# A scheduler's duration table, two groups of side work placed later, and the value products of stick-breaking attention issued for two query blocks at a time

## The chip, the cores and the metric

The kernel runs on one core of a Trainium2 chip. The metric is the device time of one execution in microseconds (us), given as the median of the runs shown. Five instruction streams matter: TensorE (PE in the profile, with its weight loads as PEld), VectorE (DVE), ScalarE (ACT), GpSimd (POOL) and SyncE (SP), whose queue carries most of the loads.

## What is computed

A sequence of 1024 tokens of width 1024, in float32, goes through three layers. Layer one is a short convolution with gates. Layer two is stick-breaking attention with 16 heads of 64, in query blocks of 128:

```
z = einsum(q, k) * inv_sqrt_d ;  mask = kpos < qpos          # strictly below
log_beta = log_sigmoid(z) ;  log_1m_beta = where(mask, log_beta - z, 0)
suffix = cumsum(log_1m_beta, reverse) - log_1m_beta
a = where(mask, exp(log_beta + suffix), 0) ;  out = a @ v
```

Layer three is a block with two attentions side by side, a sliding window (8 heads) and a differential attention (4 heads, two softmaxes each, a norm behind), merged by gates, and a feed-forward part with a convolution and a Gelu. Each layer has shifts, scales and gates that come from a vector-matrix product with a conditioning vector (`c @ w`); layer three has six of them in `w_ada` (1024 x 6144): `shift1, scale1, gate1, shift2, scale2, gate2`. The first three are used around the attentions, the last three around the feed-forward part.

## The kernel before, in words

Activations are kept transposed (channels on the partitions) in two halves of 512 tokens. Each large product is made of three TensorE passes over a high and a low part of both operands. A weight piece (128 x 512) is loaded by SP (`wr`), its high part is cast on ACT (`wh`), its low part is a subtraction on DVE (`wl`); an activation tile gets its high part on ACT and its low part on DVE (`split_to`). The products write PSUM tiles `pj` (`pv` where the tokens stand on the partitions).

The order on every engine is fixed when the program is built, by a planner (`Sched`). The main line calls one projection after another (`run_q0`, `run_bo0`, ...) and these are TensorE's filler. Everything else is a side task, a Python generator, that yields what it waits for; `turn` lets the side tasks whose time has come put their instructions in between. Time is the planner's own: `note` (line 153) adds to a clock for each engine a duration worked out from the operation and its width. So a duration in `note` changes no instruction but moves many. `until(cond)` runs side tasks alone, without filler, until a condition holds. Flags such as `"attn2"` live in the planner only; on the chip there are the semaphores that follow from the data.

Side tasks that matter here:

- `stick` (line 1068): a unit is one head of a head pair p and one query block i; with n = i+1 key blocks. It multiplies scores (`z`), takes two sigmoids on ACT (`om`, `be`, or `ob` for both where n is at most 4), a scan on DVE over `om` (a running product), a product of `be` and `om` on DVE, n transposes on TensorE (`tr`), copies on ACT (`aT`), and then, when both heads of the pair are there, the products with the values into `o`: 64 columns of the array for each head, key blocks 0 to i, the last one (the diagonal) with 127 rows instead of 128. The units of half 0 (i = 0 to 3) run beside `run_q0` to `run_z1a`, those of half 1 (i = 4 to 7) beside `run_bo0`, `run_z1`, `run_c0`, `run_g0`. `until(("stick", 0))` stands ahead of `run_bo0`.
- `swa` and `diff`: the two attentions of layer three. A unit of `diff` makes two softmaxes (a custom DVE instruction that adds the distance and reduces, shown as CUSTOM_DVE_ANT_0 in the trace and ISA in the order; an exponential on ACT), combines them on DVE (`p`), transposes, multiplies. After the fourth block of a head comes a norm (`sub_norm`: `sq`, `sm`, a square root on ACT, `rb`) and the split of `od`. `until(("attn2", 1))` stands ahead of `run_br1`, the first projection that reads `od` of half 1; `run_g1` and `run_up0` are the filler before it.
- `gemv_side`: the products with the conditioning vector, a load `mw` on SP and an accumulation `acc` on DVE for each 128 x 512 piece. For `w_ada` that is 96 pieces, one per 1.8 us of planned time (`EVERY`), in one go.
- `combine`: sums and differences of the tiles of two halves (`T`, `xn`) ahead of `run_up1`.
- `act_side`: loads (`al`) and splits of the down projection's inputs, from the start of `run_up1` on.
- `weight_sums`: adds blocks of weights by DMAs on the POOL queue.

Of the kernel before, what the change touches and what calls it, by code (L numbers as in the profile page):

```python
# [16 lines left out]
D = 1024  # L17
S = 1024
HT = 512
# [24 lines left out]
N_SP = 8  # L44
T_XT = 55.0
EVERY = 1.8
N_Z = 2
N_G = 7
M_BR = 5
# [8 lines left out]
class Sched:  # L58
# [91 lines left out]

        self.in_bank[ap.tensor.name][0] = None

    def note(self, eng, op, out, args, extra=0.0):
        ready = self.ready
        names = [a.tensor.name for a in args]
        self.seq += 1
        start = max([self.clk[eng]] + [ready.get(n, 0.0) for n in names])
        o = out.tensor.name
        n = out.free_size()
        lat = 0.1  # L160
        if eng == "pe":
            start = max(start, self.fresh.pop(o, 0.0))
            if op == "transpose":
                d = 0.113 if self.t > 30.0 else 0.213
            elif args[0].dtype == F32R:
                d = n / 2400 if n >= 256 else n / 600
            elif args[0].dtype == BF16:
                d = n / 2400
            elif n == 1:
                d = 0.2 if self.t > 30.0 else 0.37  # L170
            else:
                d = n / 600 if args[0].free_size() == 128 else n / 1070
            d += 0.0026
        elif eng == "act":
            d = n / 1400 + 0.155 + extra
        elif eng == "dve":
            fast = op in ("tensor_scalar", "tensor_copy") and all(a.space == out.space != bass.MemoryType.PSUM
                                                                  for a in args)
            d = n / (1920 if fast else 960) + 0.06
            if op == "reciprocal":  # L180
                d += n / 192
        else:
            d = 1.05 if eng == "pool" else 0.55
            nbytes = n * out.shape[0] * 4
            t = max(self.clk["dma"], start + d) + nbytes / 360e3
            self.clk["dma"] = t
            lat = t + 1.8 - start - d
        self.clk[eng] = start + d
        for nme in names + [o]:
            self.last[nme] = self.seq, max(start + d + lat, self.last.get(nme, (0, 0.0))[1])  # L190
        ready[o] = max(ready.get(o, 0.0), start + d + lat) if eng != "pe" else start + d + lat
        if eng != "pe":
            for nme in names:
                b = self.in_bank.get(nme)
                if b is not None:
                    b[0] = max(b[0] or 0.0, start + d)
# [29 lines left out]
class Engine:  # L226
# [5 lines left out]
    def __getattr__(self, op):  # L232
        f = getattr(self.eng, op)

        def call(out, *value, **kw):
            if op == "activation":
                s = Sched.SETS.get(kw["func"])
                if s and s != self.sch.set:
                    self.sch.set = s
                    self.sch.clk["act"] += 1.28  # L240
            args = [a for k, a in kw.items() if isinstance(a, bass.AP) and k not in ("accum_out", "identity")]
            extra = 0.19 * any(isinstance(kw.get(k), bass.AP) for k in ("scale", "bias")) + 0.095 * ("accum_out" in kw)
            self.sch.note(self.name, op, out, args, extra)
            if "accum_out" in kw:
                self.sch.ready[kw["accum_out"].tensor.name] = self.sch.ready[out.tensor.name]
            if self.dry:
                return None
            if op in ("matmul", "memset"):
                return f(out, *value, **kw)  # L249
            return f(out=out, **kw)  # L250
        return call
# [13 lines left out]
def tile_body(  # L265
# [802 lines left out]
    def stick(live, half, width, rho):  # L1068
        nk = (half + 1) * HT
        kv, qs = stick_in[half]  # L1070
        st = {}

        def work(p, i, h):
            yield from arrived(kv, p)
            yield from arrived(qs, p)
            n = i + 1
            w = n * 128
            kk, vt, q = kv[p][0][h], kv[p][1], qs[p][h]
            yield kk, q
            qb = q[:, :, (i % 4) * 128:(i % 4 + 1) * 128]  # L1080
            yield from room(1 if w <= HT else 3, int(w > HT))
            if w <= HT:
                both = big([2, HT], name="ob")
                om, be = both[:, 0, :], both[:, 1, :]
            else:
                om, be = big([D], name="om"), big([D], name="be")
            for c0, c1 in CUTS[n]:
                yield from sch.a_bank()
                ps = bank("z")
                o = ps[:, 0:c1 - c0]  # L1090
                mm(o, lhsT=qb[:, 0, :], rhs=kk[:, c0:c1], start=True, stop=False)
                mm(o, lhsT=qb[:, 1, :], rhs=kk[:, c0:c1], start=False, stop=True)
                e = min(c1, w)
                act(out=om[:, c0:e], in_=ps[:, 0:e - c0], func=ACTF.Sigmoid, scale=-1.0)
                act(out=be[:, c0:e], in_=ps[:, 0:e - c0], func=ACTF.Sigmoid)
            yield om


            rev = om[:, 0:w][:, ::-1]
            vec.tensor_tensor_scan(out=rev, data0=rev, data1=cst1["begin"][:, D - w:D][:, ::-1], initial=0.0, op0=ALU.mult,  # L1100
                                   op1=ALU.add)
            vec.tensor_tensor(out=be[:, 0:w - 1], in0=be[:, 0:w - 1], in1=om[:, 1:w], op=ALU.mult)
            free(w > HT)
            yield be
            aT = yield from turn(be, n)
            free()
            got = st.setdefault((p, i), {})
            got[h] = aT
            if len(got) < 2:
                return  # L1110
            if p not in st:
                yield from sch.a_bank()
            if p not in st:
                st[p] = [bank("o"), 0]
            po = st[p][0]
            yield vt
            for kb in range(n):
                r = slice(0, 127 if kb == n - 1 else 128)
                for hh in range(2):
                    mm(po[64 * hh:64 * hh + 64, (i % 4) * 128:(i % 4 + 1) * 128],  # L1120
                       lhsT=vt[r, kb * 128 + 64 * hh:kb * 128 + 64 * hh + 64],
                       rhs=got[hh][r, kb * 128:(kb + 1) * 128], start=kb == 0, stop=kb == n - 1)
            free(2 * (w > HT))
            del st[p, i]
            st[p][1] += 1
            if st[p][1] == 3 and ("z", p, half) in flags:
                zs[p, half] = sml(name="zl")
                syn.dma_start(out=zs[p, half], in_=z_d[p, :, hs(half)])
            if st[p][1] == 4:
                o = sml(name="o")  # L1130
                z = zs.get((p, half))
                if z is None:
                    vec.tensor_copy(out=o, in_=po)
                else:
                    vec.tensor_tensor(out=o, in0=po, in1=z, op=ALU.mult)
                if z is not None and in_use[0] + R_OB <= N4:
                    flags.add(("oB", p, half))
                    sch.spawn(split_to(("oB", p, half), o))
                else:
                    store(o_d[p, :, hs(half)], o)  # L1140
                del kv[p], qs[p], st[p]
                free(3 + 2 * half)
                kv["done"].add(p)
                qs["done"].add(p)

        yield from crew(live, [(p, i, h) for p in range(8) for i in range(4 * half, 4 * half + 4) for h in range(2)],
                        work, width, lambda p, i, h: rho * 0.32 * (i + 1), lambda: flags.add(("stick", half)))
# [295 lines left out]
            combine("h2", "T", rb, xs, GS["2"], V["sh2"], 6.0)  # L1443

    def h2_side():
        while "f" not in RB:
            yield 1.0
        for j in range(NJ):
            sch.spawn(from_dram(x4_d, 0, j, RB["f"], GS["2"][:, j:j + 1], V["sh2"][:, j:j + 1], ("h2", j, 0)))
# [590 lines left out]
    with tc.manual_schedule():  # L2040
# [135 lines left out]
        def mods_2():  # L2176
# [6 lines left out]
                yield 1.0  # L2183
            V["f_conv_n"] = const.tile([128, 3 * NF], F32, name="f_conv_n")
            vec.tensor_scalar(out=V["f_conv_n"], in0=V["f_conv"], scalar1=-1.0, scalar2=None, op0=ALU.mult)
            yield from gemv_side(w_ada_2[0], 0, 6 * D, sc2, mod_2, V["b_ada"], EVERY)
            make_gs("1", "sc1", "n1_g")
            make_gs("2", "sc2", "n2_g")
            vec.tensor_scalar(out=V["gt1"], in0=V["gt1"], scalar1=0.5, scalar2=None, op0=ALU.mult)
            flags.add("mods_2")  # L2190

        def consts_2():

# [88 lines left out]
        sch.spawn(ob_load(1))  # L2282
        run_bo1()
        run_g0b()
        run_c1()
        sch.until(lambda: ("attn2", 0) in flags)
        run_br0()
# [6 lines left out]
        run_up0b()  # L2294
        run_wo1()
        run_up0c()
        sch.spawn(act_side())
        run_up1()
        ahead.update(load=AHEAD_LOAD + E_L, h=AHEAD_H + E_H, l=AHEAD_L + E_H)
        run_last()  # L2300
# [33 lines left out]
```

## Time and profile before

| what | value |
|---|---|
| median of 3 runs | 2584.52 us (2581.15 to 2585.07) |
| the profiled execution's own time | 2582.41 us |
| its span, first to last instruction | 2580.6 us |
| PE busy | 2505.5 us (97%) |
| DVE, ACT, POOL busy | 1792.8, 1255.7, 490.0 us |
| mean granted TensorE clock | 0.991 |

PE is busy nearly all the time, so the places where it is not are few and can be listed one by one. [...] In a row of the waits the engine on the left sat idle until the one behind the arrow was done. [...]

### The profile page before, as it was taken

To read this page: it belongs to the slowest core of one execution; us is meant where nothing else is said; L and a number is where in the kernel's file an instruction comes from. 1 tells how busy PE (TensorE), PEld (TensorE's weight loads), DVE (VectorE), ACT (ScalarE), POOL (GpSimd) and SP (SyncE) were. 2 spreads that over 40 slices of the span, in tenths; PEclk is the share of its full clock that TensorE was granted. 3 is DMA by queue.
4 is the path that set the end of the run, shared out by engine and by line. 5 is a ranking of instruction groups with operands and counts; after the bars stand their busy time and mean duration, and the time that the engine had idled before them with its cause. 6 is when DMAs were issued, how large, how long until landed. Compare 5 with 4: busy or idle time off the path is not lost.

```text
span 2580.6 us, 38805 instructions
## 1 busy us (share of the span) xinstructions
PE 2505.5 (97%) x13215; PEld 2057.5 (80%) x13215; DVE 1792.8 (69%) x3245; ACT 1255.7 (49%) x2529; POOL 490.0 (19%) x894
## 2 busy tenths in 40 slices
PE   7999999989999899998999999999999899999998
PEld 6888888879877677787888887888888678788887
DVE  7866666777697788986765556774666876677555
ACT  5311112555455677677664353564634634345442
POOL 0012112312101002331211321222222222221000
PEclk9999999999999999999999999999999999999999
DMA  9867869857897665775876978977886987978764
GB/s 283 264 190 201 203 214 280 235 185 249 279 274 222 204 163 157 221 192 140 250 217 160 262 209 261 260 226 220 200 237 217 237 225 235 238 225 252 226 201 130
DMA packets 541726, 570.43 MB, mean 221 GB/s; under 512 B 32910, under 2 KB 410008, under 8 KB 541528
## 3 DMA queue, kind: packets, MB, share of 16 engines
q1 hardware_dynamic: 482644, 381.99, 50.3%
q0 software_dynamic: 56528, 181.75, 25.3%
q10 hardware_dynamic: 2356, 4.21, 0.4%
q8 instruction: 104, 1.70, 0.3%
q14 instruction: 94, 0.77, 0.1%
HBM read 466.90 MB, written 186.91 MB: 253 GB/s over the span
## 4 chain that ended last, share of the span: by engine, by line
PE 65%; DVE 5%; DMA 3%; ACT 2%; issue 2%; SPq 0%; POOL 0%; DVEq 0%; ACTq 0%; POOLq 0%
PE pj L249 53%; PE o L249 4%; PE z L249 4%; PE tr L250 3%; DVE om L250 2%; PE pv L249 1%; DMA wr<-sg_d2g 1%; DVE be L250 1%; DVE wl L250 1%; DMA wr<-in_b_w_out_dram 1%; DVE ob L250 1%; DVE act L250 0%; DVE fa L250 0%; ACT om L250 0%; ACT be L250 0%
## 5 line engine op out<-in xcount | busy, mean ns | idle before, releaser
L249 PE MATMUL pj<-act,wh 128*128 128x512 f32 (+1 forms) x5680 | 1783.0, 395 | 26.2 <-DVE act L250 16.8
L249 PEld LDWEIGHTS pj<-act,wh 128*128 128x128 f32 x5680 | 1046.2, 189 | 256.8 <-DVE act L250 22.9
L249 PE MATMUL pj<-act,wl 128*128 128x512 f32 (+1 forms) x2840 | 1113.7, 392 | 0.0
L249 PEld LDWEIGHTS pj<-act,wl 128*128 128x128 f32 x2840 | 536.2, 189 | 123.1 <-DVE wl L250 1.3
L250 DVE TENSOR_TENSOR wl<-wr,wh 128x512 fp32r<-128x512 f32 x714 | 476.4, 679 | 169.7 <-ACT wh L250 156.2
L250 ACT CAST wh<-wr 128x512 fp32r<-128x512 f32 x714 | 425.8, 617 | 177.6 <-PE pj L249 41.8
L250 POOL COPY paced<-wl 128x1 f32<-128x1 f32 x256 | 114.7, 448 | 881.6 <-DVE wl L250 840.9
L250 ACT COPY aT<-tr 128x512 f32<-128x512 f32 (+3 forms) x272 | 128.7, 501 | 162.0 <-PE tr L250 159.6
L249 PE MATMUL z<-kd,qs 128*128 128x512 f32 (+2 forms) x704 | 166.4, 350 | 1.7 <-DVE o L250 0.7
L250 DVE SCALAR_TENSOR_TENSOR acc<-mw,silu_c,acc 128x512 f32<-128x512 f32 x196 | 146.5, 748 | 2.7 <-DMA mw<-in_a_mod_w_dram 0.3
L249 PEld LDWEIGHTS z<-kd,qs 128*128 128x128 f32 x704 | 113.7, 190 | 19.4 <-issue 7.2
L250 DVE TENSOR_TENSOR_SCAN om<-om,begin 128x640 f32<-128x640 f32 (+3 forms) x64 | 120.6, 1885 | 10.2 <-ACT om L250 10.2
L249 PEld LDWEIGHTS o<-aT,vp 128*64 128x64 f32 (+2 forms) x1440 | 99.9, 149 | 22.8 <-issue 14.5
L249 PE MATMUL o<-aT,vp 128*64 128x128 f32 (+2 forms) x1440 | 116.3, 280 | 0.4 <-ACT aT L250 0.4
L250 ACT COPY u<-pj 128x512 f32<-128x512 f32 x46 | 27.0, 588 | 157.8 <-PE pj L249 80.1
L250 ACT ACTIVATE p<-p,t 128x256 f32<-128x256 f32 (+7 forms) x128 | 81.3, 636 | 20.7 <-DVE t L250 20.5
L250 ACT ACTIVATE sq<-xn 128x512 f32<-128x512 f32 x48 | 30.6, 637 | 110.6 <-DVE xn L250 110.5
L250 ACT ACTIVATE om<-z 128x384 f32<-128x384 f32 (+2 forms) x128 | 69.3, 542 | 22.6 <-PE z L249 19.0
L249 PE MATMUL pj<-wh,act 128*128 128x256 f32 x448 | 79.9, 281 | 0.0
L250 PE MATMUL tr<-ident,be 128*128 128x128 f32 x416 | 61.1, 283 | 18.1 <-DVE be L250 17.7
L250 PEld LDWEIGHTS tr<-ident,be 128*128 128x128 f32 x416 | 47.3, 143 | 32.4 <-DVE be L250 20.7
L250 DVE TENSOR_TENSOR be<-be,om 128x639 f32<-128x639 f32 (+3 forms) x64 | 66.2, 1034 | 6.7 <-ACT sq L250 0.5
(252 smaller groups left out, 2757.5 us busy)
## 6 DMA issues: line engine op xcount, KB each, us to landing
wr<-in_w_in_dram SPq DMA_DIRECT2D x136, 256.0 KB
mw<-in_w_ada_dram SPq DMA_DIRECT2D x96, 256.0 KB
wr<-in_a_w_in_dram SPq DMA_DIRECT2D x80, 256.0 KB
al<-dn_d SPq DMA_DIRECT2D x77, 256.0 KB
wr<-in_w_up_dram SPq DMA_DIRECT2D x66, 256.0 KB
sw_d<-in_w_down_dram POOLq DMA_DIRECT2D x48, 352.0 KB, 5.0
wr<-in_b_w_qz_dram SPq DMA_DIRECT2D x64, 256.0 KB
qs<-q_d SPq DMA_DIRECT2D x64, 256.0 KB
```

Source lines behind the costliest of these rows:

```text
L249: return f(out, *value, **kw)
L250: return f(out=out, **kw)
```

## The change

Four edits. (1) In `note` the scan costs n/470 + 0.04 us instead of n/960 + 0.06, a `scalar_tensor_tensor` with a scalar from memory 0.068 us more, a `tensor_tensor_reduce` (the custom instruction) 0.03 us more. (2) `w_ada` is taken in two goes: the first three vectors as before, the last three after the flag `attn1` (set behind `run_g0b`), one piece per 3.0 us. (3) In `stick` a block whose four transposed tiles (both heads of i and of its neighbour i^1) are not all there goes no further; the last of the four issues both blocks' products in one row, the even block from key block 0 up to its diagonal, the odd one from its diagonal down to 0, so that the two diagonals stand next to each other. (4) `act_side` starts 60 us of planned time later.

```diff
-    def note(self, eng, op, out, args, extra=0.0):
+    def note(self, eng, op, out, args, extra=0.0, scalar=None):
...
             if op == "reciprocal":
                 d += n / 192
+            elif op == "tensor_tensor_scan":
+                d = n / 470 + 0.04
+            elif op == "scalar_tensor_tensor" and isinstance(scalar, bass.AP):
+                d += 0.068
+            elif op == "tensor_tensor_reduce":
+                d += 0.03
...
-            got = st.setdefault((p, i), {})
-            got[h] = aT
-            if len(got) < 2:
+            st.setdefault((p, i), {})[h] = aT
+            if any(len(st.get((p, k), ())) < 2 for k in (i, i ^ 1)):
                 return
...
-            for kb in range(n):
-                r = slice(0, 127 if kb == n - 1 else 128)
...
+            for k in (i & ~1, i | 1):
+                got = st.pop((p, k))
+                order = range(k, -1, -1) if k % 2 else range(k + 1)
+                for kb in order:
+                    r = slice(0, 127 if kb == k else 128)
...
-            yield from gemv_side(w_ada_2[0], 0, 6 * D, sc2, mod_2, V["b_ada"], EVERY)
+            yield from gemv_side(w_ada_2[0], 0, 3 * D, sc2, mod_2, V["b_ada"], EVERY)
...
+            yield from wait("attn1")
+            yield from gemv_side(w_ada_2[0], 3 * D, 6 * D, sc2, mod_2, V["b_ada"], EVERY_2)
+            make_gs("2", "sc2", "n2_g")
...
-        sch.spawn(act_side())
+        sch.spawn(act_side(), 60.0)
```

TensorE's row in `stick`, half 1, before: the scores of a unit (`z_10847`, `z_10852`, seven key blocks) and, further down, its own transposes (of `be_10846`), with one block's products with the values between them.

```order
L249 MATMUL z_10847<-kd_10086,qs_10092 128x512 x2
L249 MATMUL z_10852<-kd_10086,qs_10092 128x384 x2
...
L249 MATMUL o_10785<-aT_10807,vp_10089 64x128
L249 MATMUL o_10785<-aT_10870,vp_10089 64x128
...
L250 MATMUL tr_10904<-ident,be_10800 128x128 x4
L250 MATMUL tr_10912<-ident,be_10800 128x128 x3
L249 MATMUL z_10919<-kd_10085,qs_10091 128x512 x2
...
L250 MATMUL tr_10933<-ident,be_10846 128x128 x4
```

The same place of the changed program: the scores of a unit of seven blocks (`z_10674`, `z_10679`) and its transposes (of `be_10673`).

```order
L256 MATMUL z_10674<-kd_10156,qs_10162 128x512 x2
L256 MATMUL z_10679<-kd_10156,qs_10162 128x384 x2
...
L256 MATMUL o_10764<-aT_10604,vp_10160 64x128
L256 MATMUL o_10764<-aT_10609,vp_10160 64x128
...
L256 MATMUL o_10764<-aT_10692,vp_10160 64x128
L256 MATMUL o_10764<-aT_10725,vp_10160 64x128
...
L257 MATMUL tr_10792<-ident,be_10673 128x128 x4
```

Between a unit's last score and its first transpose stood 12 products `pj`, 13 transposes, 2 scores of 512 and 2 more, and 12 products `o`; now 18 `pj`, 16 transposes, 2 scores of 512 and 2 of 384, and 22 `o` in one row, of blocks 4 and 5.

VectorE's row at the start of `run_up1`, before: the splits (`act<-T`, `act<-xn`) that TensorE's next products wait for, and among them those of `act_side` (`act<-al`).

```order
L250 TENSOR_TENSOR act_20952<-al_20853,act_20952 128x512
L250 TENSOR_TENSOR wl_21016<-wr_20916,wh_20984 128x512
L250 TENSOR_TENSOR act_20954<-T_4540_20492,act_20954 128x512
L250 SCALAR_TENSOR_TENSOR T_4561_20605<-T_4561_20605,act_18409 128x512
L250 TENSOR_TENSOR T_4561_20605<-T_4561_20605,act_18409 128x512
L250 TENSOR_TENSOR act_20961<-al_20861,act_20961 128x512
L250 TENSOR_TENSOR act_20972<-al_20867,act_20972 128x512
L250 TENSOR_TENSOR act_20991<-al_20880,act_20991 128x512
L250 SCALAR_TENSOR_TENSOR fa_21008<-y_4652_21005,f_conv_n,fa_21008 128x511
L250 SCALAR_TENSOR_TENSOR fa_21008<-y_4652_21005,f_conv_n,fa_21008 128x510
L250 TENSOR_TENSOR act_21010<-al_20894,act_21010 128x512
L250 TENSOR_TENSOR act_21018<-T_4541_20502,act_21018 128x512
```

The changed program from the same point (`y` is the sum that stands just ahead of the rows above).

```order
L257 TENSOR_TENSOR y_4635_20980<-pj_20959,v_20957 128x512
L257 TENSOR_TENSOR act_20944<-T_4539_20503,act_20944 128x512
L257 TENSOR_TENSOR wl_20991<-wr_20911,wh_20962 128x512
L257 SCALAR_TENSOR_TENSOR T_4564_20635<-T_4564_20635,act_17851 128x512
L257 TENSOR_TENSOR T_4564_20635<-T_4564_20635,act_17851 128x512
L257 SCALAR_TENSOR_TENSOR fa_20983<-y_4635_20980,f_conv_n,fa_20983 128x511
L257 SCALAR_TENSOR_TENSOR fa_20983<-y_4635_20980,f_conv_n,fa_20983 128x510
L257 TENSOR_TENSOR act_20985<-T_4540_20513,act_20985 128x512
```

The first two splits of `T` behind `y` stood in places 3 and 12; now they stand in places 1 and 7 behind it, with no `al` between.

TensorE's row at the end of `diff`, half 1, before: the last products with the values (`o_19090`), the last norm (`sm`, `rb`) and the first product of `run_br1` (`pj_19433`), with the filler of `run_up0` (`pj_19293`, `pj_19328`) between them.

```order
L249 MATMUL o_19090<-aT_19263,vp_18726 128x128 x8
L249 MATMUL pj_19293<-act_18015,wh_19185 128x512 x2
...
L250 MATMUL sm_19344<-ident,sq_19316 128x128 x4
L249 MATMUL pj_19328<-act_18015,wh_19208 128x512 x2
...
L250 MATMUL rb_19410<-ident,t_19402 128x128 x4
L249 MATMUL pj_19328<-act_18411,wh_19296 128x512 x2
L249 MATMUL pj_19328<-act_18411,wl_19333 128x512
L249 MATMUL pj_19433<-act_15863,wh_19331 128x512 x2
```

The changed program: `pj_19052` is the last filler, `pj_19441` the first product of `run_br1`; the last head's products go to `o_19283`.

```order
L256 MATMUL pj_19052<-act_18078,wl_19057 128x512
L257 MATMUL sm_19194<-ident,sq_19175 128x128 x4
...
L257 MATMUL rb_19247<-ident,t_19240 128x128 x4
L257 MATMUL tr_19260<-ident,p_19147 128x128 x4
...
L256 MATMUL o_19283<-aT_19270,vp_18498 128x128 x6
...
L257 MATMUL tr_19371<-ident,p_19309 128x128 x4
L256 MATMUL o_19283<-aT_19370,vp_18498 128x128 x8
L257 MATMUL sm_19405<-ident,sq_19402 128x128 x4
L257 MATMUL rb_19424<-ident,t_19422 128x128 x4
L256 MATMUL pj_19441<-act_15790,wh_19055 128x512 x2
```

Before, filler (64 rows of `pj`) stands between the first product into `o_19090` and the last `rb`, and a little behind it; in the changed row everything from `sm_19194` to the last `rb_19424` (28 rows: the norm of head 2, and the scores, transposes, products and norm of units 4 to 7 of the last head) stands behind the last filler product, with no filler in it.

## Rows read from the trace of the kernel before

**Rows 1.** The page, part 1: busy time, share, instructions.

```profile
PE 2505.5 (97%) x13215; PEld 2057.5 (80%) x13215; DVE 1792.8 (69%) x3245; ACT 1255.7 (49%) x2529; POOL 490.0 (19%) x894
```

**Rows 2.** Stretches: length, busy time of PE, PEld, DVE, ACT, POOL, clock, DMA.

```profile
690.00:879.00 189.00, 186.22 (x1125) 143.61 (x1124) 151.87 (x251) 107.48 (x256) 20.01 (x37) 1.00 0.86 258
879.00:894.00 15.00, 8.51 (x52) 6.91 (x52) 12.53 (x13) 10.68 (x28) 1.08 (x2) 0.77 0.69 234
894.00:1215.00 321.00, 300.71 (x2233) 250.93 (x2234) 270.20 (x339) 235.53 (x517) 67.28 (x93) 0.98 0.63 171
1215.00:2035.00 820.00, 817.80 (x4158) 674.68 (x4158) 517.89 (x1208) 423.90 (x854) 192.35 (x373) 1.00 0.80 227
1831.70:1865.90 34.20, 34.20 (x189) 29.23 (x188) 21.10 (x51) 21.08 (x35) 9.48 (x18) 1.00 0.79 195
2035.00:2056.00 21.00, 12.83 (x41) 8.70 (x41) 18.13 (x31) 10.98 (x20) 4.11 (x6) 0.76 0.91 227
```

**Rows 3.** PE's waits, 893 to 1215 us: total, times, longest.

```profile
PE tr L250 <- DVE be L250: 12.6, 18, 2.0
PE pv L249 <- ACT be L250: 3.1, 1, 3.1
```

**Rows 4.** Groups by form on DVE: busy, mean ns, idle before.

```profile
L250 DVE TENSOR_TENSOR_SCAN om<-om,begin 128x1024 f32<-128x1024 f32 x16 | 36.6, 2285 | 1.0 <-ACT om L250 1.0
L250 DVE SCALAR_TENSOR_TENSOR acc<-mw,silu_c,acc 128x512 f32<-128x512 f32 x196 | 146.5, 748 | 2.7 <-DMA mw<-in_a_mod_w_dram 0.3
```

**Rows 5.** PE's timeline around the value products: start, duration.

```profile
1161.06 0.65 PE L250 MATMUL tr<-ident,be 128*128 128x128 f32 x4
1161.64 1.31 PE L249 MATMUL o<-aT,vp 128*64 128x128 f32 x20
1162.89 0.44 PE L250 MATMUL tr<-ident,be 128*128 128x128 f32 x2
```

**Rows 6.** PE's timeline at the change from half 0 to half 1.

```profile
884.78 1.33 PE L250 MATMUL tr<-ident,be 128*128 128x128 f32 x5 [3.71 <-DVE be L250]
```

**Rows 7.** PE's timeline at the start of run_up1.

```profile
2036.46 0.62 PE L249 MATMUL pj<-act,wh 128*128 128x512 f32 x2
2036.92 0.39 PE L249 MATMUL pj<-act,wl 128*128 128x512 f32 x1
...
2039.96 0.50 PE L249 MATMUL pj<-act,wh 128*128 128x512 f32 x1 [2.42 <-DVE act L250]
...
2045.75 0.80 PE L249 MATMUL pj<-act,wh 128*128 128x512 f32 x1 [4.54 <-DVE act L250]
```

**Rows 8.** DVE's timeline at the same place.

```profile
2041.15 1.90 DVE L250 TENSOR_TENSOR act<-al,act 128x512 fp32r<-128x512 f32 x3
...
2045.01 0.68 DVE L250 TENSOR_TENSOR act<-T,act 128x512 fp32r<-128x512 f32 x1
```

**Rows 9.** Groups by form on ACT, the whole span.

```profile
L250 ACT ACT_TABLE_LOAD x44 | 56.5, 1283 | 3.5 <-PEq L2321 1.7 <-PE pj L249 1.0
L250 ACT ACTIVATE p<-p,t 128x768 f32<-128x768 f32 x8 | 7.5, 933 | 1.5 <-DVE t L250 1.5
```

**Rows 10.** DVE's timeline in diff's last units.

```profile
1841.62 0.68 DVE L250 CUSTOM_DVE_ANT_0 p<-z,DD 128x512 f32<-128x512 f32 x1
1842.22 0.08 DVE L250 DVE_READ_ACCUMULATOR2_ANT t<- 128x1 f32 x1
...
1844.72 1.15 DVE L250 SCALAR_TENSOR_TENSOR p<-p,t,p 128x896 f32<-128x896 f32 x1
...
1846.70 1.28 DVE L250 SCALAR_TENSOR_TENSOR p<-p,t,p 128x1024 f32<-128x1024 f32 x1
...
1859.21 0.69 DVE L250 TENSOR_REDUCE t<-sm 128x4 f32<-128x512 f32 x1 [2.63 <-PE sm L250]
```

**Rows 11.** ACT's timeline in diff's last units.

```profile
1856.00 0.59 ACT L250 COPY od<-o 128x512 f32<-128x512 f32 x1 [0.84 <-PE o L249]
1856.49 0.60 ACT L250 ACTIVATE sq<-o 128x512 f32<-128x512 f32 x1
```

More of the change, by code (lines that the diff above doesn't have):

```diff
@@ L46 @@
 EVERY = 1.8
+EVERY_2 = 3.0
 N_Z = 2
@@ L242, in call @@
             extra = 0.19 * any(isinstance(kw.get(k), bass.AP) for k in ("scale", "bias")) + 0.095 * ("accum_out" in kw)
-            self.sch.note(self.name, op, out, args, extra)
+            self.sch.note(self.name, op, out, args, extra, kw.get("scalar"))
             if "accum_out" in kw:
@@ L1116, in work @@
             yield vt
-            for kb in range(n):
-                r = slice(0, 127 if kb == n - 1 else 128)
[L1119 to L1126, printed above, removed]
+            for k in (i & ~1, i | 1):
[3 more added lines that the diff above has]
+                    r = slice(0, 127 if kb == k else 128)
+                    for hh in range(2):
+                        mm(po[64 * hh:64 * hh + 64, (k % 4) * 128:(k % 4 + 1) * 128],
+                           lhsT=vt[r, kb * 128 + 64 * hh:kb * 128 + 64 * hh + 64],
+                           rhs=got[hh][r, kb * 128:(kb + 1) * 128], start=kb == order[0], stop=kb == order[-1])
+            free(4 * (w > HT))
+            st[p][1] += 2
+            if st[p][1] == 2 and ("z", p, half) in flags:
                 zs[p, half] = sml(name="zl")
@@ L1445, in h2_side @@
     def h2_side():
-        while "f" not in RB:
+        while "f" not in RB or "2" not in GS:
             yield 1.0
@@ L2185, in mods_2 @@
             vec.tensor_scalar(out=V["f_conv_n"], in0=V["f_conv"], scalar1=-1.0, scalar2=None, op0=ALU.mult)
-            yield from gemv_side(w_ada_2[0], 0, 6 * D, sc2, mod_2, V["b_ada"], EVERY)
+            yield from gemv_side(w_ada_2[0], 0, 3 * D, sc2, mod_2, V["b_ada"], EVERY)
             make_gs("1", "sc1", "n1_g")
-            make_gs("2", "sc2", "n2_g")
             vec.tensor_scalar(out=V["gt1"], in0=V["gt1"], scalar1=0.5, scalar2=None, op0=ALU.mult)
             flags.add("mods_2")
+            yield from wait("attn1")
+            yield from gemv_side(w_ada_2[0], 3 * D, 6 * D, sc2, mod_2, V["b_ada"], EVERY_2)
+            make_gs("2", "sc2", "n2_g")
         def consts_2():
@@ L2284, in tile_body @@
         run_g0b()
+        flags.add("attn1")
         run_c1()
```

## The prediction

> **What bounds the kernel now.** I read the page's busy times first: TensorE is busy 2505.5 us of a span of 2580.6 [rows 1], so 75.1 us of idle time are all that a better order can win back; the rest can only change by what the products themselves cost. Then I took the table of stretches and subtracted TensorE's busy time from the length of each [rows 2]. Idle are: 189.0 - 186.2 = 2.8 us in the second part of half 0 of the stick-breaking attention; 15.0 - 8.5 = 6.5 us at its end; 321.0 - 300.7 = 20.3 us beside its half 1; 820.0 - 817.8 = 2.2 us through the whole of the two attentions of layer three; 21.0 - 12.8 = 8.2 us at the start of `run_up1`. That is 40 of the 75; the other 35 lie at the start, the end and in places that no edit aims at. The waits say what ends the idle time: in half 1 it is 18 waits, together 12.6 us and none above 2.0, of a transpose for the product of `be` and `om` on VectorE [rows 3]. Many small waits for one kind of instruction mean an order in which the transposes stand a little too early, not an engine that is too slow: VectorE is busy 270.2 of 321 us there (84%).
>
> All sums below are against the profiled execution, 2582.41 us, which is 2.1 below the median of the runs.
>
> **1. The planner's durations.** The old rule gives a scan of 1024 columns 1024/960 + 0.06 = 1.13 us; the trace shows 2.285 [rows 4]; the new rule gives 2.22. So a unit's transposes were placed about 1.2 us too early, and the longest waits are of that size. In the changed order more of TensorE's other work stands between a unit's last score and its first transpose: in the example of the two fences, 18 products at the step of 0.70 us for three (two of `wh` and one of `wl`, from 2036.46 to 2036.92 and as much again by half [rows 7]) make 4.2 us instead of 2.8, and with the transposes, scores and value products, at 0.11 to 0.23 us each, about 9.2 us instead of 6.5. A lead longer by 2.5 us covers waits of up to 2.0. Where the planner's durations already fit (1215 to 2035 us) TensorE idles 2.2 us in 820 [rows 2]. But VectorE's 84% remain, and 3.1 us of waits on ACT [rows 3] are not this edit's, so I let 5 of the 20.3 stay. Value taken: -15, and -3 for the clock, whose 0.98 [rows 2] over 321 us means some 6 us too much. Ends: 0 (the waits return in another place) and -20.
>
> **2. The w_ada pieces leave half 0.** 48 accumulations of 0.748 us [rows 4] are 36 us of VectorE's time that move from before 800 us to about 1345 to 1490 us, one per 3.0 us of planned time. In half 0 VectorE was busy 151.9 of 189 us and TensorE idle 2.8 [rows 2]; I take -2 (0 to -2.8). Where they go, 48 loads of 256 KB (12.6 MB) are added; the DMA share is 0.80 over that stretch already and VectorE is at 63%. TensorE there has weight pieces loaded ahead as its cover. [...] I take +1.5, which also pays for the changed order at the start (-2 to +6).
>
> **3. Two blocks in one group.** A block's value products use half of the array's columns per matmul, and entering and leaving this form costs time: from the transposes at 1161.06 to the next ones at 1162.89 are 1.83 us for 4 transposes and 10 pairs of products, which at 0.109 us each would be 1.53 [rows 5]. [...] 64 groups become 32: 32 x 0.24 = 7.8. Value -7.5; ends -8 and 0 (the half blocks wait for each other, and what is saved turns into waiting). The reversed odd block saves nothing by itself that I can see.
>
> [...]
>
> **4. The splits of `al` out of the way.** At 2039.96 and 2045.75 TensorE waits 2.4 and 4.5 us for splits of `T` [rows 7], while VectorE does splits of `al` in front of them: three in a row take 1.90 us [rows 8], 0.60 each beyond the first. Six stand in the row of before, 3.6 us, and none in the changed one. What is late next is the chain of `T` itself, so not all of the 8.2 us go; the clock of 0.76 [rows 2] gives a part back. Value -4.5 (-2 to -9).
>
> **5. The loss: the filler runs out ahead of `run_br1`.** In before, TensorE is busy every one of the 34.2 us in which the last head's products and norm are done (1831.70 to 1865.90 [rows 2]), because 64 rows of `pj`, 32 steps of 0.70 us, 22.4 us, stand between them; their own work is the rest, 11.8 us. In the changed order there is no filler from `sm_19194` to `rb_19424` and TensorE has only some 13 us of its own. How long does the chain last? By before's durations:
> - ACT first, from the last filler product: `od` and `sq` 1.2 [rows 11], three table loads at 1.28, four exponentials of about 0.93 [rows 9] with 0.2 of read-out, a square root 0.2: 9.5, of which 1.2 lie ahead of the hole, 8.3.
> - units 4 and 5: reciprocals 0.3, the combination 1.0, transpose, copy and product 2.3: 3.6.
> - units 6 and 7 on VectorE: eight softmax instructions of 0.68 with 0.08 of read-out [rows 10], 6.1; two scalings 1.4; two combinations 1.15 and 1.28 [rows 10]; small ones 1.0; the score ahead 0.9: 11.9.
> - transposes, copy, products, `od`, `sq`, `sm`, the reduction of 0.69 [rows 10], small ones, `rb`: 5.9.
> [...]
>
> Together 31.5, against the 34 of before: 31.5 - 13 = 18.5 us of idle time, and after it and in it the half clock. The end of half 0 shows what a broken stretch does: 0.77 over 15 us [rows 2]. That is +4 for the 13 us of matmuls partly at half clock. Value +22; ends 12 (ACT's first part overlaps, since its exponentials needn't wait for the norm) and 28 (every hop queues, all at half clock).
>
> [...]
>
> **6. The change of halves.** TensorE idles 6.5 us between 879 and 894, the longest wait 3.7 us for `be` [rows 6]. The products that now wait for the fourth tile stand behind the filler as well: +3 (0 to +6).
>
> Sum: -18 - 2 - 7.5 - 4.5 = -32; +22 + 3 + 1.5 = +26.5; in all about -5.5 or -6, so 2576.5 for the profiled execution and with the 2.1 **2578 us** for the median.
>
> **Rivals.** (a) Slower: the hole decides. If every one of its stages queues, it costs 28 instead of 22, the change of halves 6, and the waits of half 1 give back only 10: -24 + 28 + 6 + 1.5 = +11.5, 2596 us. It decides from the point at which hole and halves exceed 32. For it: a chain through four engines seldom runs at the sum of its durations; against it: VectorE and ACT are free of filler's splits there. Chance 0.25. (b) More gained: the hole costs 12, since the exponentials go ahead of the norm and before's 34 us contain queueing behind splits of weights, and half 1 loses all 20 us: -35 + 12 + 3 + 1.5 = -18.5, 2566 us. Chance 0.25. (c) The durations don't do what they are for: with VectorE at 84%, the waits of half 1 turn up behind later units, and 0 to 5 of the 18 us come back: 2578 + 13 to 18, about 2594 us. For it: a queue that is 84% full; against it: 2.2 us idle in the next stretch, whose VectorE is at 63%, which is not the same load. Chance 0.12. (d) Table loads. ACT's order holds 57 instead of 44; 13 x 1.283 [rows 9] is 16.7 us. If a third of them stand on a path from scores to scan, +5, 2583 us, no change. ACT is at 49% [rows 1], so mostly hidden. Chance 0.06. [...]
>
> **How the numbers follow.** The likeliest case keeps 0.32, with a range of its own from 2572 to 2585. The range reaches from rival (b)'s half-way gain to (a)'s time: **2560 to 2597**. A measurement of this kernel tells 0.2%, 5.2 us, from no change: faster is below 2579.3, slower above 2589.7. Of the likeliest case six tenths (0.19) are faster, the rest (0.13) no change; (b) is faster; (a) and (c) are slower but for 0.11 of the 0.37 between them, which is no change, as (d) is. Faster 0.44, no change 0.30, slower 0.26.
>
> **What would show it.** In the profile after: TensorE's idle time between 894 and 1215 falls from 20 to about 5 and the waits for `be` from 18 to a few; products into `o` stand in rows of 10 to 30, with half as many changes of form; at the start of `run_up1` no split of `al`, idle 4 instead of 8.2; and, new, a hole of 15 to 25 us, mostly ended by VectorE and ACT, ahead of the first product of `run_br1`, with a clock below 0.9. I am wrong if that hole is under 8 or over 30 us, if the waits of half 1 stay, or if the stretch with the moved pieces (about 1345 to 1490) shows waits for DMA.

## The result and the profile after

The changed kernel takes 2604.56 us (2604.36 to 2604.78), against 2584.8 us for the kernel before on the same chip: the ratio is 1.0078, with an interval of 1.0061 to 1.0096. It is slower by 20 us; 2578 was forecast, and the range ended at 2597.

The stretches of the kernel after, to be read as [rows 2]. The stretch beside half 1 has the bounds of before; the change of halves (now 871 to 893 us), the hole and the start of `run_up1` are taken where they now lie:

```profile
690.00:871.00 181.00, 181.00 (x1125) 147.70 (x1124) 129.28 (x208) 108.35 (x262) 20.03 (x38) 1.00 0.78 218
871.00:893.00 22.00, 17.48 (x112) 14.23 (x112) 19.93 (x20) 16.44 (x40) 0.49 (x1) 0.84 0.74 212
894.00:1215.00 321.00, 298.78 (x2140) 255.35 (x2138) 249.79 (x332) 219.96 (x481) 68.11 (x103) 0.96 0.67 182
1846.40:1883.40 37.00, 21.72 (x120) 19.13 (x119) 21.39 (x63) 19.99 (x34) 8.45 (x15) 0.82 0.45 106
2056.00:2077.00 21.00, 16.28 (x53) 11.14 (x52) 17.42 (x31) 10.69 (x19) 3.71 (x6) 0.84 0.70 134
```

TensorE idles 22.2 us beside half 1 of the stick-breaking attention, where it idled 20.3, and the clock there is 0.96 instead of 0.98 (the granted clock as a share of the full one; read over single microseconds of this stretch it falls to 0.50, as from 1024 to 1026 us). The hole ahead of `run_br1` is 37 us long with 15.3 us idle and a clock of 0.82. In the second part of half 0 TensorE no longer idles at all (2.8 us before), at the change of halves it idles 4.5 us (6.5 before), at the start of `run_up1` 4.7 (8.2 before).

The whole span as a sum of idle time, from TensorE's busy time in stretches with the same bounds in both traces (before, after, in us); behind the hole the work of the kernel after lies some 20 us later:

| stretch | before | after | |
|---|---|---|---|
| 0 to 545 | 15.1 | 16.7 | +1.6 |
| 545 to 893 | 15.0 | 10.6 | -4.4 |
| 893 to 1240, beside half 1 | 21.0 | 25.4 | +4.4 |
| 1240 to 1800 | 2.2 | 3.0 | +0.8 |
| 1800 to 1900, the hole | 0.0 | 15.3 | +15.3 |
| 1900 to 2110 | 8.2 | 4.7 | -3.5 |
| 2110 to the end | 13.6 | 19.5 | +5.9 |

That is 75.1 against 95.1 us, 20.0 of the 22.0 by which the span grew. The other 2 are in TensorE's busy time (2505.5 to 2507.5 us), where two things nearly cancel. The products with the values cost 6.9 us less, by their line in the page before

```profile
L249 PE MATMUL o<-aT,vp 128*64 128x128 f32 (+2 forms) x1440 | 116.3, 280 | 0.4 <-ACT aT L250 0.4
```

and after,

```profile
L256 PE MATMUL o<-aT,vp 128*64 128x128 f32 (+2 forms) x1440 | 109.4, 278 | 0.7 <-ACT aT L257 0.6
```

and the clock's mean fell from 0.991 to 0.984. Products take longer where it is lower: three of 512 columns (two with `wh`, one with `wl`) stand 0.70 us apart at a clock of 1.00 (1013.57 to 1014.27 in the changed kernel) and 1.28 us at 0.50 (1224.93 to 1226.21). That these two together make the 2 us is not shown by a run of its own.

TensorE's waits beside half 1 (893 to 1215 us) changed their shape, not their sum. Before, 18 short waits for `be` [rows 3]; now:

```profile
PE tr L257 <- DVE be L257: 10.3, 6, 4.5
PE pv L256 <- ACT wh L257: 4.6, 1, 4.6
```

Six waits for `be` instead of 18, the longest 4.5 instead of 2.0 us. And VectorE waits for TensorE more (the totals stand at e9). TensorE's timeline at two of the merged rows:

```profile
1004.58 3.50 PE L256 MATMUL o<-aT,vp 128*64 128x128 f32 x60
...
1023.02 1.30 PE L257 MATMUL tr<-ident,be 128*128 128x128 f32 x6 [4.53 <-DVE be L257]
...
1198.34 3.50 PE L256 MATMUL o<-aT,vp 128*64 128x128 f32 x60
```

and VectorE's beside them:

```profile
1008.18 0.69 DVE L257 TENSOR_TENSOR o<-o,zl 128x512 f32<-128x512 f32 x1 [4.38 <-issue]
1008.79 1.48 DVE L257 TENSOR_TENSOR_SCAN om<-om,begin 128x640 f32<-128x640 f32 x1
...
1201.89 0.69 DVE L257 TENSOR_TENSOR o<-o,zl 128x512 f32<-128x512 f32 x1 [6.59 <-PE o L256]
```

The reader is to see the order of events: the product with `z` (`o<-o,zl`) stands at the head of VectorE's row while TensorE is in a row of 60 records, 3.4 us without a score or a transpose. VectorE idles 4.4 us with a scan right behind. The trace names no releaser for this wait (`issue`), but the product starts 0.2 us behind the end of the row. Afterwards VectorE has no pause until 1050. That TensorE's 4.5 us at 1023 are the price of it is argued from this order, not measured.

In the hole TensorE waits on one chain through VectorE and ACT (a fourth wait, 1.23 us for `sq` on ACT, is left out here):

```profile
1846.82 1.55 PE L256 MATMUL z<-kd,qs 128*128 128x384 f32 x8
1853.90 1.09 PE L257 MATMUL rb<-ident,t 128*128 128x128 f32 x4 [5.53 <-DVE t L257]
...
1870.86 3.55 PE L257 MATMUL tr<-ident,p 128*128 128x128 f32 x15 [6.18 <-DVE p L257]
...
1882.99 0.73 PE L257 MATMUL rb<-ident,t 128*128 128x128 f32 x4 [2.23 <-DVE t L257]
```

### The profile page after: what moved, and what is told of

It is laid out like the page before. It is cut to its first block, busy times and chain, and to the rows that moved or that the text cites. A ratio compares the mean times of both kernels' runs of the same rounds, so it can differ in the third digit from the quotient of the medians.

```text
span 2602.6 us, 38853 instructions
## 1 busy us (share of the span) xinstructions
PE 2507.5 (96%) x13215; PEld 2073.2 (80%) x13215; DVE 1793.8 (69%) x3244; ACT 1270.5 (49%) x2542; POOL 484.6 (19%) x893
## 4 chain that ended last, share of the span: by engine, by line
PE 88%; DVE 6%; DMA 2%; ACT 2%; issue 1%; SPq 0%; POOL 0%; DVEq 0%; ACTq 0%; POOLq 0%
PE pj L256 73%; PE o L256 4%; PE z L256 4%; PE tr L257 4%; PE pv L256 2%; DVE om L257 1%; DVE act L257 1%; DVE fa L257 1%; DMA mw<-in_a_mod_w_dram 1%; DVE p L257 1%; DVE wl L257 1%; PE sm L257 1%; DMA wr<-sg_d2g 1%; DVE be L257 1%; ACT L257 0%
## 5 line engine op out<-in xcount | busy, mean ns | idle before, releaser
L256 PEld LDWEIGHTS pj<-act,wh 128*128 128x128 f32 x5680 | 1049.0, 189 | 261.0 <-DVE act L257 20.5
L256 PE MATMUL z<-kd,qs 128*128 128x256 f32 (+2 forms) x704 | 162.9, 348 | 2.4 <-ACT aT L257 2.3
L256 PE MATMUL o<-aT,vp 128*64 128x128 f32 (+2 forms) x1440 | 109.4, 278 | 0.7 <-ACT aT L257 0.6
```

## The experiments

All were timed beside the kernel before. A ratio is to that kernel, with its interval; a trace is of one execution, within 2.6 us of the median except for e4 (its fastest, 2578.29 us) and e5 (its slowest, 2583.14 us); "idle beside half 1" is 347 us less TensorE's busy time between 893 and 1240. The later start of `act_side` has no run of its own; every kernel made from the changed one has it. First three edits alone, and the changed kernel without one.

**e1: the durations alone** (the `note` part of the diff).

> The kernel before with the planner's new durations alone (scan, scalar_tensor_tensor, custom instruction). Theory W (the waits of half 1 are transposes placed too early): TensorE's idle time beside half 1 (about 894 to 1215 us) falls from 20 to 5 to 8 us and the time by 12 to 18 us, to 2567 to 2573. Theory V (VectorE's own queue is the bound there, the layer norm's instructions among the scans): the many small waits go, fewer and longer ones take their place, idle stays at 17 to 23 us, time 2580 to 2588. Its order has no hole ahead of run_br1, so neither expects one.

2588.45 us, ratio 1.0020 (1.0010 to 1.0029). Idle beside half 1 is 18.1 us against 21.0 (15.8 in the stretch of the expectation, 894 to 1215, between the theories and nearer to V): theory V's shape, and the time just above its range. The waits for `be` (893 to 1215) are 7 instead of 18, 8.1 us together, but one of 4.0 us for ACT came, and 3.9 us of idle time between 1800 and 1900. Theory W fell.

**e2: the move of w_ada's second half alone.**

```diff
-            yield from gemv_side(w_ada_2[0], 0, 6 * D, sc2, mod_2, V["b_ada"], EVERY)
+            yield from gemv_side(w_ada_2[0], 0, 3 * D, sc2, mod_2, V["b_ada"], EVERY)
...
+            yield from wait("attn1")
+            yield from gemv_side(w_ada_2[0], 3 * D, 6 * D, sc2, mod_2, V["b_ada"], EVERY_2)
```

> The kernel before with the move of the second half of w_ada alone (its last three vectors after attn1, one piece per 3.0 us). Its order has 10.5 us of TensorE work without filler ahead of run_br1. Theory H (this edit alone makes the hole): idle of 14 to 18 us there and half the clock, 2584.5 + 18 to 24 = 2602 to 2608, less up to 3 for the quieter half 0. Rival (the hole needs the new durations as well, here it is mostly covered): below 8 us idle there, 2580 to 2590.

2594.38 us, ratio 1.0041 (1.0026 to 1.0056). The hole is there, 15.4 us idle between 1800 and 1900 at a clock of 0.88, as theory H has it; the time is below its range, in part because idle beside half 1 fell to 15.2.

**e3: the merged rows alone** (the `stick` part of the diff).

> The kernel before with the merged rows of value products alone. Theory G (only the entries and exits count): 32 groups fewer at 0.24 us, -7.8 us, 2577, idle beside half 1 as before (20 us). Theory M (the long rows hold up the scores behind them and VectorE stands behind the product with z until they end): idle and half clock beside half 1 grow by 5 to 15 us and eat the gain, 2582 to 2592. No hole ahead of run_br1 for either.

2598.72 us, ratio 1.0057 (1.0040 to 1.0074): 15 us slower than before, more than theory M allowed. Idle beside half 1 is 30.0 us, one wait alone 10.8 us (`pv` for `wh`); the products with the values cost 110.7 instead of 116.3. The entries are saved and more is lost. (Theory M's reason, VectorE behind the product with `z`, is not the whole of it: see the table below.)

**e4: the changed kernel without the move.**

> The changed kernel with the move of w_ada's second half undone. Theory H: the hole ahead of run_br1 goes (its order has filler there) and with it 22 to 26 us: 2579 to 2583, with the waits of half 1 as in the changed kernel (22 us idle). Rival (the hole's idle time turns up elsewhere, since VectorE and ACT are as late): idle of 8 us or more between 1800 and 2060, 2590 to 2600.

2583.55 us, ratio 0.9997 (0.9988 to 1.0006): theory H, just above its range. The hole is gone (1.4 us idle between 1800 and 1900), and the kernel is 21 us faster than the changed one; beside half 1 it idles 20.5.

**e5: the move at another pace.** To tell the moved work from the order that it brings about:

```diff
-EVERY_2 = 3.0
+EVERY_2 = 4.0
```

> The changed kernel with one number changed: a piece of w_ada's second half per 4.0 us of planned time instead of 3.0. Its order is the same up to the flag attn1; behind it, filler of run_up0 stands again between the last head's products and norm. Theory T (the hole is a tipping point of the planner: some units fall behind a gate of the tile pool, and not the moved additions themselves): the idle time ahead of run_br1 falls from 15 to below 4 us, the half clock there goes, 2604.6 - 20 to 26 = 2579 to 2585. Rival (VectorE's extra 36 us delay the attention by themselves): still 10 us or more idle between 1780 and 1900, 2596 to 2603.

2578.45 us, ratio 0.9983 (0.9974 to 0.9993): theory T, just below its range. The same work is still moved, and TensorE is busy all through the place of the hole:

```profile
1800.00:1900.00 100.00, 100.00 (x481) 82.86 (x480) 65.10 (x131) 55.07 (x92) 26.68 (x47) 1.00 0.83 217
```

So the hole costs about 2604.56 - 2578.45 = 26 us (21 by e4), and it is a tipping point of the order and not the price of 48 additions. The trace of the changed kernel says the same: its last addition starts at 1624 us, over 200 us ahead of the hole.

```profile
L257 DVE SCALAR_TENSOR_TENSOR acc<-mw,silu_c,acc x196: 740/747/755, 11.9 to 1624.3; 128x512 f32<-128x512 f32 x196
```

In e5 the last one starts later still, at 1680 us, and there is no hole.

**e6: less work on VectorE, same order.** In-place instructions of `xn`, `sq` and `z` beside half 1 are done on 64 columns; the other 448 are left out:

```diff
+            if (self.name == "dve" and self.sch.t > LIGHT[0] and self.sch.t < LIGHT[1]
+                    and out.tensor.name.split("_")[0] in ("xn", "sq", "z") and out.free_size() == 512
+                    and out.tensor.name == kw["in0"].tensor.name):
+                out = out[:, 0:64]
...
```

> The changed kernel, same order, with 29 in-place VectorE instructions beside half 1 done on 64 of their 512 columns (8 of xn in the layer norm, 14 sums of squares, 7 products of z); their results are wrong for the rest. It takes some 17 us off VectorE between 890 and 1215 us, 6 of them between 1008 and 1050, and leaves scans and be alone. Theory V (VectorE's amount of work beside half 1 is what the transposes wait for): idle between 1000 and 1100 falls from 12.3 to 6 us or less, beside half 1 from 22 to 15 or less, time 2604.6 - 8 to 14 = 2590 to 2597. Theory W (it is the order and the latency of each unit): idle there stays above 18, 2601 to 2605.

2597.85 us, ratio 1.0052 (1.0036 to 1.0069): 6.7 us faster than the changed kernel, between the two theories. VectorE's busy time fell by 13.2 us (1793.8 to 1780.6), not by 17. Idle beside half 1 is 23.1 us, so TensorE got 2.3 us back there: its waits for `be` fell from 13.5 to 9.4 us (893 to 1240), and one of 3.2 us for ACT came. The amount of VectorE's work plays a part, but alone it does not decide.

**e7: the changed kernel without the merged rows.**

> The changed kernel with the merged rows of value products undone; the hole ahead of run_br1 is in its order too. Theory G (the rows save 8 us of entries and exits and do no harm): 2610 to 2614. Theory M (the rows cost more in waits than they save, as they did alone): 2590 to 2600, with 4 to 12 us less idle beside half 1 than the changed kernel's 22.

2596.23 us, ratio 1.0051 (1.0036 to 1.0066): theory M. Without the rows it is 8.3 us faster, though the products with the values cost 119.8 us instead of 109.4; idle beside half 1 is 12.0 instead of 25.4.

**e8: the changed kernel without the durations.**

> The changed kernel with the planner's new durations undone; no hole in its order. If the durations help beside half 1 and the rows harm there (theory M): many small waits for be again, 22 to 28 us idle beside half 1 as with the rows alone, 2588 to 2598. If the durations harm and the rows help: idle beside half 1 below 15, 2570 to 2580.

2580.45 us, ratio 0.9990 (0.9980 to 0.9999). No hole, and 31.4 us idle beside half 1: the rows harm, and the durations soften that. The time is below what theory M gave, just above its rival's range; its clock (0.991) stayed up, and idle time is lower elsewhere (81.6 us in all against 95.1).

The idle time beside half 1 in us, by what the order was planned with:

| | single blocks | merged rows |
|---|---|---|
| old durations | 21.0 (before), 15.2 (e2) | 30.0 (e3), 31.4 (e8) |
| new durations | 18.1 (e1), 12.0 (e7) | 20.5 (e4), 25.4 (after), 24.1 (e5) |

Rows against single blocks: 9.0, 16.2, 2.4, 13.4 us more (e3 to before, e8 to e2, e4 to e1, after to e7). New durations against old: 2.9, 3.2, 9.5 and 6.0 to 7.3 us less.

In the two kernels with rows and old durations the longest single wait is not for VectorE. In e8 it is this one of 12.2 us for a weight cast on ACT (10.8 in e3, 4.6 in the changed kernel, 2.1 in e2, none in before and e7):

```profile
1161.00 0.58 PE L250 MATMUL pv<-wh,act 128*128 128x256 f32 x1 [12.20 <-ACT wh L251]
```

In the 20 us ahead of that cast (1140 to 1160.4) ACT is busy but for 0.9 us, and half of that time goes to table loads:

```profile
L251 ACT ACT_TABLE_LOAD x8 | 10.3, 1283 | 0.1
```

In the changed kernel, 10 of the 16 table loads between 893 and 1240 us, of 1.28 us each, stand where ACT goes from the sigmoids (`be` is the last) to `t` and the exponentials (`p`), or back from `p` to `om`. This is what the prediction's rival (d) is about. In all, ACT loads tables 57 times in the changed kernel, as forecast, 44 times in before and 42 in e13, the fastest. No run changes the table loads alone, so how much of the rows' harm is theirs stays open. In the changed kernel that wait (at 1144 us) follows a pause of 5.6 us in which ACT has no transpose, behind another row of 60 records, and two table loads.

**e9: let other work pass the waiting product.** From e5, one line:

```diff
             if st[p][1] == 4:
+                yield po
                 o = sml(name="o")
```

> The changed kernel with one piece per 4.0 us (as e5_every4) and one line more: stick yields the PSUM tile before VectorE's product with z is put into its row, so that other VectorE work goes ahead while TensorE is still in the long row of value products. Theory R (the rows of 44 or 60 records, 3.1 to 3.5 us, hold VectorE at the head of its row and starve it beside half 1): VectorE's idle time before o falls from 24 to below 8 us between 893 and 1240, TensorE's idle beside half 1 from 21 to 14 or less, 2578.5 - 6 to 14 = 2564 to 2572. Rival (any new order deals the same waits out afresh): idle beside half 1 between 17 and 25, 2574 to 2584.

2566.69 us, ratio 0.9940 (0.9924 to 0.9957). Theory R by its time. VectorE's waits for `o` between 893 and 1240 (total, times, longest), in the changed kernel:

```profile
DVE o L257 <- PE o L256: 19.7, 6, 6.6
DVE o L257 <- issue: 4.4, 1, 4.4
```

in the kernel before:

```profile
DVE o L250 <- PE o L249: 9.8, 5, 3.4
```

and in e9:

```profile
DVE o L257 <- PE o L256: 10.2, 4, 3.6
```

They fell from 24 to 10 (not below 8, as expected), and TensorE's idle time beside half 1 from 24.1 in e5 to 11.8. But only 4.1 of these 12.3 us are waits for `be`. TensorE's waits in e5 (893 to 1240):

```profile
PE tr L257 <- DVE be L257: 12.5, 6, 4.5
PE pv L256 <- ACT wh L257: 4.6, 1, 4.6
PE tr L257 <- ACT be L257: 2.4, 1, 2.4
PE z L256 <- ACT aT L257: 2.3, 1, 2.3
```

In e9 the waits for `be` are 8.4 us and those for ACT 0.8. ACT's table loads in this stretch fell from 16 to 12 in the new order. So the line gains what theory R says, and a part of it by way of ACT, which is not separated.

**e10: four units alive** (and a piece per 4.5 us).

> As e9_late_o, with four units of half 1 alive at a time instead of three and a piece per 4.5 us. Theory R: the fourth unit's scores give VectorE work during the rows, idle beside half 1 below 12, 2558 to 2568. Rival: more units in VectorE's row only make each later, 2574 to 2584.

2567.27 us, ratio 0.9941 (0.9926 to 0.9955), idle beside half 1 13.6: neither theory, the fourth unit changes nothing.

**e11 and e12: the same line without merged rows**, in e9 and in the kernel before.

> As e9_late_o without the merged rows (one block's products at a time). Its order has filler ahead of run_br1. Theory R: VectorE loses little at rows of 20 to 32 records, so idle beside half 1 is as in e7_no_merge (12 us) and the time 2570 to 2577; against e9_late_o it then lacks the 8 us of entries, and comes out 2 to 8 us slower. If the rows still harm, it is the faster of the two.

> The kernel before with the one line of e9_late_o alone. Theory R: at most the 11 us that VectorE idles before o can count, and small rows starve it little: 2578 to 2584. Rival (the line itself is what helps, rows or not): 2570 to 2576.

e11: 2583.23 us, ratio 0.9995 (0.9985 to 1.0004), idle beside half 1 15.2, where e7 without the line had 12.0. e12: 2590.53 us, ratio 1.0029 (1.0019 to 1.0039), idle 22.7 where before had 21.0. The times miss what theory R gave by 6 us each on the slow side. Its core holds: where the rows are short the line gains nothing, where they are long it gains 12 us. And e12 shows how far a new order alone can move the time: the line changes little beside half 1 (1.7 us), and the kernel is 7 us slower, 3.9 of it idle time between 1800 and 1900. A difference of that size between two orders says little by itself.

**e13 and e14: e9 without the durations, and without the move.**

> As e9_late_o with the planner's old durations. If the durations help beside half 1: many small waits for be again, idle there (893 to 1240) 16 to 24 us against e9's 12, time 2572 to 2580. If they don't: idle within 3 us of e9's, 2563 to 2570.

> As e9_late_o with all of w_ada's pieces in half 0, as before. If the move is worth what it takes off VectorE in half 0 (step 2 of the prediction): idle between 545 and 893 larger by 2 to 5 us than e9's, the time 2567 to 2573. If the hole's removal leaves nothing of the move: within 2 us of e9, 2565 to 2569.

e13: **2556.83 us, ratio 0.9896 (0.9880 to 0.9913)**, the fastest version, and below both expectations. Beside half 1 it idles 14.2 us, much as e9, but in the old shape. The stretch and its waits for `be` in e9:

```profile
893.00:1240.00 347.00, 335.17 (x2425) 286.70 (x2424) 282.25 (x367) 245.20 (x535) 86.13 (x124) 0.99 0.69 190
...
PE tr L257 <- DVE be L257: 8.4, 3, 5.2
```

and in e13:

```profile
893.00:1240.00 347.00, 332.81 (x2469) 278.58 (x2469) 288.41 (x432) 249.03 (x570) 72.66 (x111) 1.00 0.68 186
...
PE tr L251 <- DVE be L251: 11.9, 18, 1.1
```

Eighteen waits of at most 1.1 us (and one of 1.7) leave the clock at 1.00, three with one of 5.2 do not (0.99). Against e8, which lacks the line and has the pace of 3.0, e13 is 24 us faster and idles 17 us less beside half 1; the 12.2 us wait for the cast is gone, and ACT's table loads there are 9 instead of 21. In all of e13 TensorE idles 62.2 us (span 2553.2, busy 2491.0) against 68.5 in e9 (span 2564.7, busy 2496.2), and its clock is 0.994 against 0.991. e14: 2581.85 us, ratio 0.9994 (0.9985 to 1.0003). Idle between 545 and 893 is 15.0 against e9's 10.9, as expected; the rest of the 15 us lies in other places (idle 76.5 in all, clock 0.985) and was not expected.

## Why the prediction was wrong

**Step 1 failed: "Value taken: -15, and -3 for the clock".** The wrong sentence is that many small waits mean "an order in which the transposes stand a little too early", so that a later place takes them away. They did go, 18 became 6 (7 in e1). But TensorE's idle time fell only by 3 to 10 us in the four comparisons of the table, and the time followed in one of them only: e4 is 15 us below e3, some of it from the later `act_side`. e5 is 2 us below e8; e7 is 2 us above e2, e1 5 us above before, and e9 10 us above e13, which has the old durations. What came in the place of the small waits is few long ones, 4.5 us in the changed kernel and 5.2 in e9, and in or right behind those the clock falls (0.50 from 1024 to 1026 us, behind the wait that ends at 1023): by the clock over single microseconds between 893 and 1240, TensorE was at 0.50 for 27 us in the changed kernel and for 10 before; in e13 the clock over the whole stretch is 1.00. So -3 for the clock had the wrong sign too. My end of 0 for this term ("the waits return in another place") was the right case, and rival (c) with its 0.12, 2594 us, was the nearest to it in its mechanism; no rival reached the measured time. (The new durations also go with more idle time ahead of 545 us, 16.3 to 18.3 us in the ten kernels that have them, against 14.5 to 15.1 in those that don't, but for e3 with 17.1.)

**Step 3 had the wrong sign: -7.5 forecast, +8.3 measured (after against e7), +15 alone (e3).** Idle time beside half 1 grew in all four comparisons of the table. The time did not follow everywhere: e4 is 5 us faster than e1 (some of it from the later `act_side`), and with the late product the rows gain 17 us (e9 against e11). Its price was right: 6.9 us off the products with the values are 0.22 for each of 32 groups; the 0.24 a group that the sum takes is shown by no run. What I set at nothing is what stands behind a row: for 2.6 to 3.5 us (rows of 44 records take 2.6, one at a clock that was 0.50 to begin with 3.1, rows of 60 take 3.5) neither ACT nor VectorE gets a score or transpose, and VectorE, whose next instruction is the product with `z`, stands idle ahead of it, 4.4 and 6.6 us at the two rows shown above, with a scan right behind it at the first. The bound that I wrote, 0, for half blocks that wait for each other, looked at TensorE's row alone. e9 against e5 fits this (12 us of idle time less, at both engines), e11 and e12 fit that it needs long rows. But two thirds of TensorE's 12 us were waits for ACT, and table loads (rival (d)) are a second cause that no run rules out; the share of each stays open. These two terms are most of the miss: I had 25.5 us of gain from them, and beside half 1 there are 4.4 us more idle time and a lower clock.

**Step 5 was right.** +22 forecast; e4 prices the hole at 21 us and e5 at 26. Its parts were off in opposite directions, so that the sum came out so well is partly luck: 15.3 us of idle time instead of 18.5, and by the clock of 0.82 over 37 us up to 6.7 us (0.18 x 37) for the half clock instead of 4. No run shows the 1.8 us that the 31.5 hold for the hops between engines; in the trace of before `p` on ACT starts 0.04 us behind the end of the `t` that it waits for (1838.10), and `tr` 0.06 behind the end of `be` (1163.79). That the moved additions don't cause it by their weight, but through the order, the prediction did not say. Why a pace of 3.0 tips the order and 4.0 doesn't was read in the orders only, and no run isolates it.

**Steps 2, 4 and 6.** Half 0 was right: -2 forecast, -2.8 measured (690 to 871 us), and e4 and e14, without the move, wait 3.5 and 3.6 us for `ob` there again. The change of halves shrank by 2.0 us where I had +3. At `run_up1` -3.5 for -4.5. The pieces' new place is not the one I gave: the additions run from 1436 to 1624 us and not from 1345 to 1490. It cost +0.8 (1240 to 1800), and no wait of TensorE there is for a DMA; the +1.5 of the sum was a guess of mine, which no run shows. The move without its hole is worth more than the 0.5 us that I gave it: 5 us by e5 against e4, 15 by e9 against e14, of which 4 where I looked.

**Not foreseen:** 5.9 us more behind 2110, where TensorE waits for `y` four times in place of once,

```profile
PE pj L256 <- DVE y L257: 8.2, 4, 2.9
```

and 1.6 at the start. Such waits differ from order to order: between 2110 and 2500 e13 idles 0.3 us and e9 5.8. Their cause stays open, and so does how much of e13's gain on e9 (10 us) is such luck.

## What to carry to other kernels

The price of a wait lies in what stands behind it in its engine's row: here VectorE idled 4.4 us ahead of the product with `z`, with a scan right behind it. Before instructions of one engine are put together in a longer row, look at whose row is headed by the result, and let other work pass it (here one line, 12 us with long rows and nothing with short ones). Correct durations in a planner need not make a better order; judge them by the trace, and prefer many short waits to few long ones where the clock follows (1.00 in e13, 0.99 in e9 and 0.96 in the changed kernel, between 893 and 1240 us). A change that moves the whole order should be tried part by part: here the best version keeps the merged rows and the move, at another pace, without the durations.

## What was not expected of the hardware

Spread waits cost the clock nothing here: 18 waits of up to 1.1 us in 347 us left the granted clock at 1.00 (e13). The clearest pair is e2 and e11, with the same idle time of 15.2 us beside half 1:

```profile
893.00:1240.00 347.00, 331.82 (x2440) 275.71 (x2439) 288.46 (x400) 253.85 (x559) 79.46 (x109) 1.00 0.65 177
...
893.00:1240.00 347.00, 331.84 (x2391) 278.54 (x2388) 280.78 (x367) 248.77 (x537) 76.02 (x111) 0.97 0.64 178
```

In e2, the first row, no wait is longer than 2.1 us and the clock is 1.00; in e11 the longest is 3.9 us and the clock 0.97. The hole made 21 to 26 us out of 15.3 us of idle time.
